# A two-layer decoder trunk on Trainium2: first norm vector by matrix products, first tile's halves taken apart, memory rows transposed once for both layers

## The chip, the core and the metric

The kernel runs on one core of a Trainium2 chip. The engines that work side by side are TensorE (PE: matrix products, and transposes as products with an identity), VectorE (DVE), ScalarE (ACT), GpSimd (POOL), and the DMA queues of SyncE (SP), ACT and POOL. The metric is the device time of one execution in microseconds, as the median of several runs. Before the change it is 1396.72 us (three runs, 1395.12 to 1397.05).

## What is computed

512 tokens of width 1024 go through two layers. Each layer is a mixer, a cross-attention into 256 memory tokens and a SwiGLU feed-forward block, and each of these stands between two RMS norms. The mixer of layer 0 is an attention with forget gates beside a short convolution; that of layer 1 is a gated linear recurrence.

```python
def rmsnorm(x, g):
    x32 = x.astype(jnp.float32)
    y = x32 * lax.rsqrt(jnp.mean(x32 * x32, axis=-1, keepdims=True) + EPS)
    return y.astype(x.dtype) * g
...
    for layer in range(DEPTH):
        h = rmsnorm(x, g_mix_pre[layer])
        ...
        x = x + rmsnorm(y, g_mix_post[layer])
        h = rmsnorm(x, g_cross_pre[layer])
        m = rmsnorm(mem, g_mem[layer])
        y = memory_cross_attention(h, m, w_xq[layer], w_xkv[layer], w_xo[layer])
        x = x + rmsnorm(y, g_cross_post[layer])
        h = rmsnorm(x, g_ffn_pre[layer])
        y = swiglu(h, w_ffn_gu[layer], w_ffn_down[layer])
        x = x + rmsnorm(y, g_ffn_post[layer])
```

The memory `mem` is the same in both layers; only the norm's gain `g_mem[layer]` (1024 numbers, one per channel) differs. All is float32.

## The kernel before

**Precision.** Every float32 product is made of three faster ones. An operand is split into a high part (a cast by ACT to the matmul's own format, `wh`, `hTh`, `mTh`) and a low part (operand minus high part, by DVE, `wl`, `hTl`, `mTl`). `mm3` (L318) adds high times high, high times low and low times high in one PSUM bank (L319 to L321).

**Layout.** The 512 tokens are four tiles `x[0]` to `x[3]` of 128 rows by 1024 channels, worked in two halves of 512 channels. `sumsq` (L218, ACT) or a DVE reduction (L242) sums the squares of a half; `rstd` (L220) makes the reciprocal root with two tiny DVE instructions (L222, L226) and a power on POOL (L230); `scaled` (L256, DVE) multiplies a half by it and by the gain. `put_T` (L299) transposes such a half in four products on PE (L303), and ACT (L312) and DVE (L313) split the result out of PSUM into `hTh` and `hTl`. The large tiles (`group`: four times 512 columns) share 14 slots.

**Order of the work.** PE takes its instructions in the order in which the code issues them. For ACT and DVE a scheduler decides the order, but for the first part of `fox` (L1198 to L1258), where they too follow the code. An engine works its list in order, so an instruction that waits holds up all behind it. All weights come over the SP queue through a ring of four buffers `st`. After a load, `pace` (L140) may let one of the `copies` go, which are transfers from DRAM to DRAM that prepare sums of the feed-forward weights (20 in each layer, planned at L677); `loads[0]` counts the loads, and a copy follows three of four loads once the count is above 0. The second operand of these sums is added by transfers of the POOL queue (L679).

**Start.** The norm's gain for the first tile comes in two ways. Half 0 is loaded as one row into `grow`, and a float32 product with a matrix `ones` (L1220, two passes in the trace) spreads it over the 128 partitions in a PSUM bank. Half 1 is loaded by SP with a transfer that writes it to all 128 partitions (`gain`, 256 KB). `warm_up` (L1176) runs products that nobody reads. Then both halves of tile 0 are transposed, and `mm_v` (L1189) makes the first products with the weights `st` (cast L1213, subtraction L1216): for the first two channel blocks "h" (high, high), "w" (high, low weights), "x" (low, high weights). Tile 1 follows after more products of tile 0.

**Memory.** In each layer `memory_rows` (L941) loads the four blocks of `mem` (L950), two by two sums their squares, and multiplies them by reciprocal root and gain (L956); the gain comes in two 256 KB transfers on the ACT queue (L107). `memory_T` (L961) returns two steps; each transposes one tile of 128 memory rows in eight products (L971) and splits them with two ACT casts (L976) and two DVE subtractions (L977). The steps run inside `half1` (L585), which makes the second half of the mixer's output projection: for each token tile 24 products, and after some of them `next` (row sums, norm) of the tile before and `transpose` of the one before that. Step 0 follows tile 0 and step 1 tile 1. `memory_kv` (L981) then needs `mTh` and `mTl`; its weights are `w_xkv`. Both layers call this at L1548 to L1549.

## Time and profile before

| what | value |
|---|---|
| median of three runs | 1396.72 us (1395.12 to 1397.05) |
| the profiled execution, its own time | 1394.71 us |
| its span, first to last instruction | 1392.9 us |
| what lies around the span | 1.8 us |
| mean granted clock of TensorE | 0.997 |
| PE busy | 1378.2 us, 99% of the span |
| DVE busy | 1116.3 us, 80% |
| ACT busy | 720.2 us, 52% |
| POOL busy | 111.1 us, 8% |
| DMA traffic | 233.61 MB, 168 GB/s on average |

The profile is one execution. A row of its timeline gives start and duration in us, the engine, the line of the code, the operation, output and inputs with shapes; "x4" is a group of four that ran one after the other, and "[1.05 <-DVE h L256]" says that the engine had been idle for 1.05 us, and what ended that. A row of its windows gives a stretch of time, then for PE, PEld, DVE, ACT and POOL the busy us with the number of instructions, the granted TensorE clock (1.00 is full), the share of the 16 DMA engines and the GB/s they moved. PE is counted as busy from start to modelled end, so a pipeline that is merely fed slowly looks busy too. 168 GB/s over the span is an average: the first 15 us move 287 GB/s.

### The profile page before, as it was taken

To read this page: it belongs to the slowest core of one execution; us is meant where nothing else is said; L and a number is where in the kernel's file an instruction comes from. 1 tells how busy PE (TensorE), PEld (TensorE's weight loads), DVE (VectorE), ACT (ScalarE), POOL (GpSimd) and SP (SyncE) were. 2 spreads that over 40 slices of the span, in tenths; PEclk is the share of its full clock that TensorE was granted. 3 is DMA by queue.
4 is the path that set the end of the run, shared out by engine and by line. 5 is a ranking of instruction groups with operands and counts; after the bars stand their busy time and mean duration, and the time that the engine had idled before them with its cause. 6 is when DMAs were issued, how large, how long until landed. Compare 5 with 4: busy or idle time off the path is not lost.

```text
span 1392.9 us, 21792 instructions
## 1 busy us (share of the span) xinstructions
PE 1378.2 (99%) x8432; PEld 1227.8 (88%) x8432; DVE 1116.3 (80%) x1801; ACT 720.2 (52%) x1175; POOL 111.1 (8%) x162
## 2 busy tenths in 40 slices
PE   8999999999999999999999999999999999999998
PEld 6778788888899999998879888888889999999886
DVE  6876678546589999989898998754558999999987
ACT  4354455534464444456664796543446444445663
POOL 1000001012010101000010000101200010000001
PEclk9999999999999999999999999999999999999999
DMA  6845452669224557567656657267822555656664
GB/s 224 277 155 159 137 181 57 202 164 177 66 92 142 163 143 196 160 241 222 195 159 210 222 181 242 73 199 163 164 67 91 166 150 151 177 168 233 205 188 144
DMA packets 156066, 233.61 MB, mean 168 GB/s; under 512 B 8549, under 2 KB 90545, under 8 KB 154938
## 3 DMA queue, kind: packets, MB, share of 16 engines
q1 hardware_dynamic: 135138, 180.25, 40.3%
q0 software_dynamic: 16928, 45.11, 15.0%
q10 hardware_dynamic: 3896, 6.86, 1.5%
q8 instruction: 66, 1.08, 0.3%
q14 instruction: 38, 0.31, 0.1%
HBM read 220.64 MB, written 57.69 MB: 200 GB/s over the span
## 4 chain that ended last, share of the span: by engine, by line
PE 95%; DVE 3%; issue 1%; DMA 1%; ACT 0%; POOL 0%; SPq 0%; DVEq 0%; POOLq 0%; ACTq 0%
PE bA L319 14%; PE bA L321 14%; PE bA L320 14%; PE bB L319 6%; PE bB L320 6%; PE bB L321 6%; PE bB L795 2%; PE bB L794 2%; PE bB L793 2%; PE bA L552 2%; PE bA L554 2%; PE bB L554 2%; PE bA L553 2%; PE bB L553 2%; PE bB L552 2%; PE bA L795 2%
## 5 line engine op out<-in xcount | busy, mean ns | idle before, releaser
L529 DVE TENSOR_TENSOR wl<-st,wh 128x1024 fp32r<-128x1024 f32 x108 | 131.4, 1222 | 99.1 <-ACT wh L528 98.1
L528 ACT CAST wh<-st 128x1024 fp32r<-128x1024 f32 x108 | 113.4, 1051 | 122.4 <-PE bA L320 70.6
L319 PE MATMUL bA<-hTh,wh 128*128 128x512 f32 (+1 forms) x448 | 171.9, 384 | 0.0
L321 PE MATMUL bA<-hTh,wl 128*128 128x512 f32 (+1 forms) x448 | 168.9, 377 | 2.3 <-DVE wl L781 2.3
L320 PE MATMUL bA<-hTl,wh 128*128 128x512 f32 (+1 forms) x448 | 168.2, 375 | 0.0
L420 ACT CAST wg<-wr 128x1024 fp32r<-128x1024 f32 x80 | 83.7, 1046 | 49.2 <-DVE wr L449 38.5
L759 ACT CAST wh<-st 128x1024 fp32r<-128x1024 f32 x76 | 74.9, 985 | 63.6 <-PE bA L795 27.0
L321 PEld LDWEIGHTS bA<-hTh,wl 128*128 128x128 f32 x448 | 84.8, 189 | 18.4 <-DVE wl L781 2.8
L421 DVE TENSOR_TENSOR wg<-wr,wg 128x1024 fp32r<-128x1024 f32 x80 | 97.4, 1217 | 0.0
L320 PEld LDWEIGHTS bA<-hTl,wh 128*128 128x128 f32 x448 | 85.0, 190 | 13.6
L319 PEld LDWEIGHTS bA<-hTh,wh 128*128 128x128 f32 x448 | 85.0, 190 | 13.4
L764 DVE TENSOR_TENSOR wl<-st,wh 128x1024 fp32r<-128x1024 f32 x76 | 86.7, 1140 | 10.1 <-ACT wh L759 10.1
L420 ACT CAST wh<-tt 128x1024 fp32r<-128x1024 f32 x40 | 42.1, 1053 | 61.5 <-DVE tt L449 61.5
L319 PE MATMUL bA<-hTq,wh 128*128 128x256 f32 x208 | 59.2, 284 | 0.0
L321 PE MATMUL bA<-hTq,wl 128*128 128x256 f32 x208 | 58.8, 283 | 0.0
L320 PE MATMUL bA<-hTq,wh 128*128 128x256 f32 x208 | 58.8, 283 | 0.0
L793 PE MATMUL bB<-wh,ya 128*128 128x512 f32 x148 | 57.6, 389 | 0.0
L794 PE MATMUL bB<-wl,ya 128*128 128x512 f32 x148 | 57.6, 389 | 0.0
L795 PE MATMUL bB<-wh,ya 128*128 128x512 f32 x148 | 57.6, 389 | 0.0
L739 DVE TENSOR_TENSOR ya<-yb,ya 128x512 fp32r<-128x512 f32 x84 | 53.9, 645 | 0.0
L793 PE MATMUL bA<-wh,ya 128*128 128x512 f32 x132 | 51.3, 389 | 0.0
L794 PE MATMUL bA<-wl,ya 128*128 128x512 f32 x132 | 51.3, 389 | 0.0
(372 smaller groups left out, 4434.8 us busy)
## 6 DMA issues: line engine op xcount, KB each, us to landing
wr<-in_w_ffn_gu_dram SPq DMA_DIRECT2D x80, 512.0 KB, 5.5
st<-t SPq DMA_DIRECT2D x40, 512.0 KB, 4.2
t<-in_w_ffn_down_dram SPq DMA_DIRECT2D x32, 512.0 KB, 5.1
st<-in_w_xkv_dram SPq DMA_DIRECT2D x32, 512.0 KB, 4.7
st<-in_w_ffn_down_dram SPq DMA_DIRECT2D x30, 512.0 KB, 3.4
st<-in_ab_w_in_dram SPq DMA_DIRECT2D x24, 512.0 KB, 4.7
y<-yr POOLq DMA_DIRECT2D x18, 512.0 KB, 4.2
t<-in_w_ffn_down_dram POOLq DMA_DIRECT2D x16, 512.0 KB, 8.4
```

Source lines behind the costliest of these rows:

```text
L319: nc.tensor.matmul(out=ps, lhsT=wh, rhs=xh, start=first, stop=False)
L320: nc.tensor.matmul(out=ps, lhsT=wh, rhs=xl, start=False, stop=False)
L321: nc.tensor.matmul(out=ps, lhsT=wl, rhs=xh, start=False, stop=last)
L420: return (lambda: nc.scalar.copy(out=to[0], in_=src), lambda: nc.vector.tensor_tensor(out=to[1], in0=src, in1=f(to[0]), op=ALU.subtract))
L421: lambda: nc.vector.tensor_tensor(out=to[1], in0=src, in1=f(to[0]), op=ALU.subtract))
L528: nc.scalar.copy(out=hi, in_=src)
L529: nc.vector.tensor_tensor(out=lo, in0=src, in1=f(hi), op=ALU.subtract)
L759: nc.scalar.copy(out=self.wt[s][0], in_=self.st[s])
L764: nc.vector.tensor_tensor(out=lo, in0=self.st[s], in1=f(hi), op=ALU.subtract)
L793: nc.tensor.matmul(out=banks[t], lhsT=yh, rhs=wh[:, jj, :], start=first and jj == 0, stop=False)
L794: nc.tensor.matmul(out=banks[t], lhsT=yh, rhs=wl[:, jj, :], start=False, stop=False)
L795: nc.tensor.matmul(out=banks[t], lhsT=yl, rhs=wh[:, jj, :], start=False, stop=last and jj == n - 1)
```

## The change

It has four parts, all in one diff.

**First gain.** Both halves of `g_mix_pre` come as rows of 2 KB, into partitions 0 and 32 of `grow`; the transfer to 128 partitions is gone. ACT casts `grow` to `growh`, DVE subtracts to `growl`, and four products with a selecting matrix `pick` put both halves into two PSUM banks. The row sums of tile 0 are issued with the DVE half ahead of `growl`.

**First tile.** Half 0 is transposed, the "h" and "w" products follow, then half 1 is transposed, then the "x" products.

**Memory.** The rows are normalised without the gain and transposed in layer 0 alone, into `raw` (a group named `mTr`). POOL's queue writes it to DRAM, `memT`, 1 MB. The gain of a layer is now one number per partition of the transposed layout (`chan`, column "gm", from 16 more rows loaded in `setup_chan`): for each of eight channel blocks ACT multiplies `raw` by it into `mTh`, and DVE makes `mTl` in one instruction. Layer 1 loads `memT` into its `raw` with one transfer on SP and has no loads of `mem`, no row sums and no transposes. The `gain` transfers of `g_mem` are gone in both layers.

**Copies.** The count of loads starts at -10, so the first of the copies follows ten loads later in layer 0.

```diff
@@ -86,10 +86,12 @@
     junk = const.tile([P, 512], BF16, name="junk")
-    grow = sbuf("grow")
-    ones = sbuf("ones", P)
+    grow, growh, growl, pick = sbuf("grow"), gains.tile([P, 512], F32R, tag="gain", name="growh"), \
+        gains.tile([P, 512], F32R, tag="gain", name="growl"), gains.tile([P, 512], F32R, tag="gain", name="pick")
     nc.vector.memset(grow, 0.0)
-    nc.vector.memset(ones, 1.0)
+    nc.vector.memset(f(pick)[:, 0:2 * P], 0.0)
+    for hf in range(2):
+        nc.vector.memset(f(pick)[32 * hf:32 * hf + 1, hf * P:hf * P + P], 1.0)
     nhalf = const.tile([P, 1], F32, name="nhalf")
@@ -160,6 +162,7 @@
         ("scw", a["ab_conv_w"][0].rearrange("j (m p) -> (j m) p", p=P)),
+        ("gm", a["g_mem"].rearrange("l (m p) -> (l m) p", p=P)),
     )
@@ -296,8 +299,8 @@
-    def put_T(hT, t, hs, bank=bankB):
-        for hf in range(2):
+    def put_T(hT, t, hs, bank=bankB, halves=range(2)):
+        for hf in halves:
             ps = bank()
@@ -938,10 +941,10 @@
-    def memory_rows(layer, gate):
-        with tc.issue_after(gate) if gate else nullcontext():
-            g = load_gain(a["g_mem"][layer])
+    memT = dram.tile([P, KT, MEM], F32, name="memT")
+    def memory_rows():
@@ -953,30 +956,46 @@
             for hf in range(2):
-                nc.vector.scalar_tensor_tensor(
-                    out=mt[hf], in0=mt[hf], scalar=r, in1=g[hf], op0=ALU.mult, op1=ALU.mult
-                )
+                nc.vector.tensor_scalar_mul(out=mt[hf], in0=mt[hf], scalar1=r)
         return mg
-    def memory_T(mg, bank):
+    def memory_T(layer, bank):
+        raw = f(group("mTr")).rearrange("p a (b c) -> p (a b) c", c=MEM)
         ghi, glo = group("mTh"), group("mTl")
...
-        def step(t):
+        if layer:
+            nc.sync.dma_start(out=raw, in_=memT)
+        else:
+            mg = memory_rows()
+        def turn(t):
             for hf in range(2):
...
                     )
-                v = ps.rearrange("p (k c) -> p k c", k=4)
-                dst = (slice(None), slice(hf * 4, hf * 4 + 4), slice(t * P, (t + 1) * P))
-                nc.scalar.copy(out=vhi[dst], in_=v)
-                nc.vector.tensor_tensor(out=vlo[dst], in0=v, in1=f(vhi[dst]), op=ALU.subtract)
-        return vhi, vlo, (lambda: step(0), lambda: step(1))
+                nc.scalar.copy(out=raw[:, hf * 4:hf * 4 + 4, t * P:(t + 1) * P], in_=ps.rearrange("p (k c) -> p k c", k=4))
+        def parts(ks):
+            for k in ks:
+                g = ch("gm", 8 * layer + k)
+                nc.scalar.mul(out=vhi[:, k, :], in_=raw[:, k, :], mul=g)
+                nc.vector.scalar_tensor_tensor(
+                    out=vlo[:, k, :], in0=raw[:, k, :], scalar=g, in1=f(vhi[:, k, :]), op0=ALU.mult, op1=ALU.subtract
+                )
+        def last():
+            turn(1)
+            nc.gpsimd.dma_start(out=memT, in_=raw)
+            parts(range(KT))
+        if layer:
+            return vhi, vlo, (lambda: parts(range(4)), lambda: parts(range(4, KT)))
+        return vhi, vlo, (lambda: turn(0), last)
@@ -1197,9 +1216,8 @@
             load_x(0)
-            nc.sync.dma_start(out=grow[0:1], in_=a["g_mix_pre"][0:1, 0:512])
-            g1 = gains.tile([P, 512], F32, tag="gain", name="gain")
-            nc.sync.dma_start(out=g1, in_=a["g_mix_pre"][0, 512:D].partition_broadcast(P))
+            for hf in range(2):
+                nc.sync.dma_start(out=grow[32 * hf:32 * hf + 1], in_=a["g_mix_pre"][0:1, hf * 512:hf * 512 + 512])
             raw = {}
@@ -1216,17 +1234,29 @@
             nc.scalar.activation(out=junk[:, 0:1], in_=nhalf, func=AF.Square)
-            g0 = bankB()
-            nc.tensor.matmul(out=g0, lhsT=ones, rhs=grow, start=True, stop=True)
-            g = g0, g1
+            nc.scalar.copy(out=growh, in_=grow)
+            g = bankB(), bankB()
+            st = stats("pre")
+            nc.vector.tensor_tensor_reduce(
+                out=sbuf("sq"), in0=x[0][:, 512:D], in1=x[0][:, 512:D], scale=1.0, scalar=0.0,
+                op0=ALU.mult, op1=ALU.add, accum_out=st[:, 1:2],
+            )
+            nc.vector.tensor_tensor(out=growl, in0=grow, in1=f(growh), op=ALU.subtract)
+            sumsq(x[0][:, 0:512], st[:, 0:1])
+            r = rstd(st)
+            for hf in range(2):
+                for i, part in enumerate((growh, growl)):
+                    nc.tensor.matmul(out=g[hf], lhsT=pick[:, hf * P:hf * P + P], rhs=part, start=i == 0, stop=i == 1)
             warm_up(WARM2)
-            r = row_stats(x[0], True)
             nc.vector.tensor_copy(out=identb, in_=ident)
...
             whi_v(0)
+            put_T(hT, 0, hs, halves=range(1))
             wlo_v(0)
-            put_T(hT, 0, hs)
-            mm_v(0, 0, "hwx")
+            mm_v(0, 0, "hw")
+            put_T(hT, 0, hs, halves=range(1, 2))
+            mm_v(0, 0, "x")
             whi_v(2)
@@ -1256,7 +1286,7 @@
                 mm_v(k0, 3)
-        loads[0] = 0
+        loads[0] = -10
         setup_chan()
@@ -1545,7 +1575,7 @@
             rglru(hT, prev, pm)
-        vhi, vlo, steps = memory_T(memory_rows(layer, pm.gate), pm.first)
+        vhi, vlo, steps = memory_T(layer, pm.first)
         pm.half1(steps)
```

At the program's start PE had this list (`grow,ones` is the gain's product, `ident,h` the transposes of `put_T`, `wh,hTh` the first weights):

```order
L1176 MATMUL bB<-ident 128x128 x13
L1220 MATMUL bB<-grow,ones 128x512
L1176 MATMUL bB<-ident 128x128 x4
L303 MATMUL bB<-ident,h 128x128 x8
L1189 MATMUL bA<-wh,hTh 128x512 x2
L1189 MATMUL bA<-wl,hTh 128x512 x2
L1189 MATMUL bA<-wh,hTl 128x512 x2
```

Now it has this:

```order
L1195 MATMUL bB<-ident 128x128 x13
L1250 MATMUL bB<-growh,pick 128x512
L1250 MATMUL bB<-growl,pick 128x512
L1250 MATMUL bB<-growh,pick 128x512
L1250 MATMUL bB<-growl,pick 128x512
L1195 MATMUL bB<-ident 128x128 x4
L306 MATMUL bB<-ident,h 128x128 x4
L1208 MATMUL bA<-wh,hTh 128x512 x2
L1208 MATMUL bA<-wl,hTh 128x512 x2
L306 MATMUL bB<-ident,h 128x128 x4
L1208 MATMUL bA<-wh,hTl 128x512 x2
```

The products for the gain are four in place of one, and the eight transposes are split in two lots of four, with the "h" and "w" products between them.

DVE at the same place, before (`x_110` is tile 0 and `x_111` tile 1; the first row makes the copy of the identity in bfloat16):

```order
L1224 CAST identb<-ident 128x128
L256 SCALAR_TENSOR_TENSOR h<-x_110,pre,bB 128x512
L256 SCALAR_TENSOR_TENSOR h<-x_110,pre,gain 128x512
L1216 TENSOR_TENSOR wl<-st,wh 128x1024
L313 TENSOR_TENSOR hTl<-bB,hTh 128x4x128 x2
L242 ISA sq,pre<-x_111 128x512
```

And now, where `x_114` and `x_115` are these tiles:

```order
L1252 CAST identb<-ident 128x128
L259 SCALAR_TENSOR_TENSOR h<-x_114,pre,bB 128x512 x2
L316 TENSOR_TENSOR hTl<-bB,hTh 128x4x128
L1234 TENSOR_TENSOR wl<-st,wh 128x1024
L316 TENSOR_TENSOR hTl<-bB,hTh 128x4x128
L245 ISA sq,pre<-x_115 128x512
```

The weights' subtraction stands between the two halves' subtractions instead of ahead of both, and the norm of both halves reads PSUM.

In layer 0, inside `half1`, DVE had this after the last update of tile 1, with what each waits for in brackets:

```order
L617 SCALAR_TENSOR_TENSOR x_111<-yb,post,x_111 128x512 [waits DVE_49]
L977 TENSOR_TENSOR mTl<-bA,mTh 128x4x128 [waits Activation_49] x2
L313 TENSOR_TENSOR hTl<-bA,hTh 128x4x128 [waits Activation_49] x2
L222 TENSOR_SCALAR pre<-pre 128x1 [waits Activation_49]
L226 SCALAR_TENSOR_TENSOR pre<-pre 128x1 [waits DVE_49,Activation_49]
L256 SCALAR_TENSOR_TENSOR h<-x_111,pre,gain 128x512 [waits Pool_49]
```

Now it is:

```order
L620 SCALAR_TENSOR_TENSOR x_115<-yb,post,x_115 128x512 [waits DVE_49]
L987 SCALAR_TENSOR_TENSOR mTl<-mTr,chan,mTh 128x256 [waits Activation_49] x8
L316 TENSOR_TENSOR hTl<-bA,hTh 128x4x128 [waits Activation_49]
L316 TENSOR_TENSOR hTl<-bA,hTh 128x4x128 [waits DMASW1_49,DVE_49,Activation_49]
L225 TENSOR_SCALAR pre<-pre 128x1 [waits Activation_49]
L229 SCALAR_TENSOR_TENSOR pre<-pre 128x1 [waits DVE_49,Activation_49]
L259 SCALAR_TENSOR_TENSOR h<-x_115,pre,gain 128x512 [waits Pool_49]
```

Two subtractions that read PSUM have become eight instructions that read `raw`. The second `hTl` now waits also for a semaphore of POOL's DMA queue (DMASW1) and for DVE's own: this tile takes the slot of `mTr`, so it waits until the write of `memT` has read it. On POOL that write stands ahead of the power of the next norm:

```order
L233 TENSOR_TENSOR post<-post,nhalf 128x1 [waits DVE_49]
L233 TENSOR_TENSOR pre<-pre,nhalf 128x1 [waits DVE_49,Pool_49]
L233 TENSOR_TENSOR post<-post,nhalf 128x1 [waits DVE_49]
L993 DMA memT<-mTr 128x2048 [waits Activation_49]
L233 TENSOR_TENSOR pre<-pre,nhalf 128x1 [waits DVE_49,Pool_49]
```

Before, the last row followed the first directly.

## The prediction

> **What bounds the kernel now.** I read first the page's chain of work that ended last, then the waits of PE, then busy time by windows.

> ```profile
> PE 95%; DVE 3%; issue 1%; DMA 1%; ACT 0%; POOL 0%; SPq 0%; DVEq 0%; POOLq 0%; ACTq 0%
> ```
> ```profile
> PE bB L303 <- DVE h L256: 2.5, 4, 1.1
> PE bA L321 <- DVE wl L781: 2.3, 2, 1.8
> ```
> ```profile
> 0.00:15.00 15.00, 10.50 (x40) 7.75 (x41) 7.96 (x18) 6.83 (x11) 3.15 (x11) 0.89 0.84 287
> 15.00:40.00 25.00, 24.73 (x120) 19.17 (x119) 17.03 (x28) 13.07 (x25) 2.01 (x2) 1.00 0.62 193
> 4.00:5.00 1.00, 1.00 (x5) 0.54 (x4) 0.72 (x3) 0.72 (x2) 0.00 (x0) 1.00 0.91 82
> 5.00:6.00 1.00, 0.82 (x5) 0.36 (x3) 0.43 (x3) 0.00 (x0) 0.52 (x1) 1.00 0.74 133
> 6.00:7.00 1.00, 0.13 (x1) 0.13 (x2) 0.75 (x1) 0.00 (x0) 0.03 (x1) 1.00 0.68 248
> 7.00:8.00 1.00, 0.58 (x5) 0.35 (x6) 0.75 (x1) 0.00 (x0) 0.00 (x0) 1.00 1.07 420
> 11.00:12.00 1.00, 1.00 (x3) 0.77 (x4) 1.00 (x3) 0.83 (x1) 0.00 (x0) 0.52 1.07 408
> 14.00:15.00 1.00, 1.00 (x5) 0.81 (x4) 0.56 (x2) 0.00 (x0) 0.76 (x1) 0.77 1.05 387
> ```

> PE carries 95% of the chain. Its waits are few: 2.5 us for the normalised rows at the very start and 2.3 us for a feed-forward weight, which this change doesn't touch. In the first 15 us PE is busy for 10.50; from 15 to 40 us for 24.73 of 25, with a clock of 1.00. So time can be won or lost in three ways only: by when PE comes to its steady work in the first 15 us, by instructions of PE that come or go, and by a new wait of PE in a place that is full now. Loads made earlier, and work taken from DVE or ACT elsewhere, are worth nothing.

> **The start.** The timeline of the first 16 us, cut to the rows that follow one another:

> ```profile
> 4.16 0.69 DVE L242 CUSTOM_DVE_ANT_0 sq<-x 128x512 f32<-128x512 f32 x1 [2.62 <-DMA x<-in_x_dram]
> 5.48 0.55 POOL L230 TENSOR_TENSOR pre<-pre,nhalf 128x1 f32<-128x1 f32 x1 [3.77 <-DVE identb L1224]
> 6.07 0.75 DVE L256 SCALAR_TENSOR_TENSOR h<-x,pre,bB 128x512 f32<-128x512 f32 x1 [0.61 <-POOL pre L230]
> 6.87 0.66 PE L303 MATMUL bB<-ident,h 128*128 128x128 f32 x4 [1.05 <-DVE h L256]
> 8.53 1.04 ACT L1213 CAST wh<-st 128x1024 fp32r<-128x1024 f32 x1 [3.58 <-DMA st<-in_ab_w_in_dram]
> 9.48 1.07 ACT L312 CAST hTh<-bB 128x512 fp32r<-128x512 f32 x2
> 9.61 1.23 DVE L1216 TENSOR_TENSOR wl<-st,wh 128x1024 fp32r<-128x1024 f32 x1 [1.72 <-ACT wh L1213]
> 10.11 0.73 PE L1189 MATMUL bA<-wh,hTh 128*128 128x512 f32 x2 [1.51 <-ACT hTh L312]
> 10.75 1.28 DVE L313 TENSOR_TENSOR hTl<-bB,hTh 128x512 fp32r<-128x512 f32 x2
> 10.89 1.11 PE L1189 MATMUL bA<-wl,hTh 128*128 128x512 f32 x2
> 12.12 0.62 ACT L218 ACTIVATE junk<-x 128x512 bf16<-128x512 f32 x1
> 13.29 1.47 POOL L230 TENSOR_TENSOR pre<-pre,nhalf 128x1 f32<-128x1 f32 x1 [7.26 <-DVE pre L226]
> 14.80 0.75 DVE L256 SCALAR_TENSOR_TENSOR h<-x,pre,bB 128x512 f32<-128x512 f32 x1 [0.45 <-POOL pre L230]
> 15.69 1.29 PE L303 MATMUL bB<-ident,h 128*128 128x128 f32 x8 [0.18 <-DVE h L256]
> ```

> What it removes: the transfer to 128 partitions. While it runs, the queues move 82, 133 and 248 GB/s in three windows, and 420 after; against 420 that is a loss of 0.81 + 0.68 + 0.41 = 1.9 us, and its own 256 KB take 0.6 us at 420. So the first weights land some 2.5 us earlier, and their cast starts at 6.0 in place of 8.53.

> What it adds ahead of the first product: `growl`, one DVE instruction of 128x512, at about the 0.69 of the row at 4.16, between the squares and the root. Some 0.1 of it lies in the wait for ACT's sum, so the norm starts at 6.07 + 0.55 = 6.6, the transposes of half 0 at 7.4, and end at 8.06; one cast (half of 1.07) ends at 8.6. The first product moves from 10.11 to 8.6. The four products for the gain take the place of an idle PE there.

> That gain of 1.5 us isn't kept, by what follows. The low weights come after the first `hTl` on DVE: 8.6 + 0.64 + 1.23 = 10.5 for the two "w" products (10.89 before). Now half 1 is transposed only after these, and ACT's list has its cast ahead of the second weights and of tile 1's squares. Step by step: two products 0.65 (between 0.45, two steps at full clock, and the 0.85 that the pairs take in the window with clock 0.52), to 11.2; four transposes 0.8 (0.66, and more at half clock), to 12.0; cast 0.54, to 12.5; second `wh` 1.04, to 13.6; squares, tiny instructions and all up to POOL's start 1.17 (from 12.12 to 13.29), to 14.7; POOL's power 1.47, to 16.2; norm to transposes 0.9 (14.80 to 15.69). Tile 1's transposes start at 17.1 in place of 15.69. All of tile 0's products fit ahead of that, and PE is full behind it, so the 1.4 us remain. **Term: +1.4.** What would hide it is other work for PE, and there is none, since tile 0 has no more channels cast. Below, the first product's whole gain of 1.5 is kept; above, a second such power or a half clock adds as much again: −1.5 to +2.9.

> The power is the largest piece. It takes 0.55 at 5.48, when DVE is idle but for a small cast, and 1.47 beside the weights' subtraction; in the new order this subtraction again lies beside it, so I take 1.47; at 0.55 the term is +0.5. [...]

> **Layer 0, memory.** The timeline around tile 1 of the output projection, a DVE instruction of 128x256 for its size, and then what POOL's transfers of 1 MB take, from the DMA issues and from the view of their line:

> ```profile
> 33.89 0.42 DVE L529 TENSOR_TENSOR wf<-st,wf 128x256 fp32r<-128x256 f32 x1
> 220.19 0.60 ACT L218 ACTIVATE junk<-bB 128x512 bf16<-128x512 f32 x1 [0.79 <-PE bB L554]
> 220.78 1.07 ACT L976 CAST mTh<-bA 128x512 fp32r<-128x512 f32 x2
> 222.09 0.15 DVE L226 SCALAR_TENSOR_TENSOR post<-post 128x1 f32<-128x1 f32 x1
> 223.57 0.75 DVE L617 SCALAR_TENSOR_TENSOR x<-yb,post,x 128x512 f32<-128x512 f32 x1
> 225.43 1.28 DVE L313 TENSOR_TENSOR hTl<-bA,hTh 128x512 fp32r<-128x512 f32 x2
> 227.77 1.42 DVE L256 SCALAR_TENSOR_TENSOR h<-x,pre,gain 128x512 f32<-128x512 f32 x2 [0.73 <-POOL pre L230]
> 229.91 1.03 PE L303 MATMUL bA<-ident,h 128*128 128x128 f32 x8
> ```
> ```profile
> yb<-y POOLq DMA_DIRECT2D x8, 1024.0 KB, 5.4
> ```
> ```profile
> DMA to landing us min/median/max: 5.0/5.4/9.4
> ```

> PE's instructions stay the same here. On DVE, step 0 loses its two subtractions, so the chain of tile 1 no longer stands behind them: its first tiny instruction follows ACT's squares, which end at 220.79, with some 0.15 for the reading of the sum: 220.95 in place of 222.09, and the update of `x` ends 1.14 earlier than 224.32, at 223.2. Then come eight instructions of 128x256 at 0.40 apart (0.42 alone): 3.2 us, to 226.4. The eight multiplications on ACT run ahead of them, from 221.85. The first `hTl` ends at 227.0. The second one waits for the write of `memT`, issued on POOL when the copies out of PSUM end, 221.85. The nearest rows are POOL's 1 MB reads, 5.4 in the median and 9.4 at most: landing at 227.3, or 231.3. With the first, `hTl` ends at 227.9, the norm follows 1.06 later as now (226.71 to 227.77), at 229.0, its first half is there at 229.75 and the second at 230.4. PE wants them at 229.91 and, four transposes on, at 230.3: **+0.1**. With the second, all is 4.0 later: +4.1. Below, 0, as PE loses no instruction. [...]

> **Layer 1, memory.**

> ```profile
> 849.76 1.88 SPq L950 DMA_DIRECT2D mem<-in_mem_dram  x4
> 856.69 0.63 ACT L531 ACTIVATE y<-ge 128x512 fp32r<-128x512 f32 x1 [0.26 <-DVE ge L1513]
> 864.79 0.39 PE L552 MATMUL bB<-wh,y 128*128 128x512 f32 x1
> 872.96 1.04 PE L971 MATMUL bB<-ident,mem 128*128 128x128 f32 x8
> 873.75 0.47 PE L552 MATMUL bA<-rh,y 128*128 128x512 f32 x1
> ```

> Two lots of eight transposes go, each 873.75 − 872.96 = 0.79 of PE's time, and the product after each is about 0.1 longer than its 0.39 neighbours: 2 × 0.9, **−1.8**. PE is full there, so this is won in full if nothing waits. The new load of 1 MB takes the place of the four loads at 849.76 and lands at 855.2 (5.4) to 859.2 (9.4). ACT's eight multiplications stand ahead of the cast of the last `y` at 856.69, which PE needs at 864.79: even from 859.2, and at the 0.54 that a cast twice their size takes, they end at 863.5 and `y` at 864.1. So this wait costs nothing; the DVE half follows later and has lost more than it gained. Bounds: −1.9 to −1.6.

> **Edits at nothing.** The copies that start ten loads later still run before the feed-forward block that reads them, and no wait of PE after 15 us is for a transfer; the cover is the whole cross-attention between. Without it a copy costs its landing, some 5 us each, once. The 16 more rows of gains and the absent 256 KB gain loads lie on ACT's queue, with nothing behind them that waits.

> **Sum.** +1.4 + 0.1 − 1.8 = −0.3. The profiled execution took 1394.71 (span 1392.9 and 1.8 around it), 2.0 less than the median of the three runs, 1396.72: the same sum gives 1394.4 on the one and 1396.4 on the other. I forecast the median: **1396.4**. A measurement of this kernel can tell about 0.2% from no change, 2.8 us, so this is no change.

> **The rivals.**

> *The first product's gain is kept* (faster). If POOL's power is short this time, and tile 1's chain goes with the first weights as it does before, the start gives −1.5 and not +1.4, and the sum is −3.2: 1393.5; with the full 2.5 us of the earlier weights −4.2: 1392.5. For it: PE waits 1.51 for `hTh` at 10.11, and that does go. Against it: the new round trip over ACT between half 0 and half 1. Chance 0.17.

> *The write of `memT` holds DVE* (slower). It lies in layer 0, where the second `hTl` waits in DVE's list with tile 1's norm behind it, and PE behind that. At the 9.4 landing the sum is −0.3 + 4.0: 1400.4. It decides from a landing 8.6 us after the issue, where the total passes +2.8. [...] Against: the median 5.4, and DMA has little to do around 220 us. Chance 0.16.

> *The clock* (about the same, or slower). In the window from 11 to 12 the clock was 0.52, and from 14 to 15 it was 0.77, so half clock lasted from 11.0 to some 14.4: 3.4 us. PE idles differently at the start, between 8.06 and 10.5. One more such stretch under full work costs half of it, 1.7: 1398.1; two 1399.8. [...] Chance 0.14, 0.07 of it slower.

> That the change doesn't do what it says is not open for layer 1: the transposes are not in PE's list.

> **How the numbers follow.** My forecast has 0.53; it lies within 0.2%, with its own range of 1395.0 to 1398.0. The rivals have 0.17, 0.16 and 0.14. Of the first 0.16 passes the bound of 2.8 us; of the second, all but little. So faster 0.16, within 0.2% 0.62, slower 0.22. The range reaches to the fast rival's lower end, 1392.5, and to the slow one's 1400.4.

> **What would show it.** In the profile after: the first product near 8.6; tile 1's transposes near 17.1 and POOL's power ahead of them near 1.5; the second `hTl` of tile 0 in layer 0 released by the transfer near 227.3 (all later by the start's shift), with a wait of PE for `h` under 0.5; no transposes of memory in layer 1, and no wait of PE there. I am wrong if PE waits in layer 0 for more than 2 us, if tile 1's transposes start before 15, or if the clock falls again after 20 us.

## The result and the profile after

The changed kernel takes 1398.23 us in the median of 22 runs (1396.77 to 1400.74); the kernel before, in as many runs beside it, takes 1395.78 (1394.71 to 1398.0). The ratio is 1.0017, with a 95% interval of 1.001 to 1.0023: 2.4 us slower. The forecast was 0.3 faster. The profiled execution of the changed kernel has a span of 1395.4 us against 1392.9, 2.4 more before rounding.

To see where they go, I took the start of each product of PE in one trace and of the same product in the other; the difference is called the shift. At 22 us it is +2.65, at 100 us +3.4, at 260 us +3.5, at 760 us +3.7, at 900 us +1.9, and at the last product +2.1 (1387.79 against 1385.71). So the start loses 2.6, something near 73 us loses 0.75, layer 1's memory wins 1.85, and the rest is small; between the last product and the end another 0.35 lies in the output's transfers.

The chain that ended last, and the first of PE's waits, of the changed kernel:

```profile
PE 91%; issue 3%; DVE 3%; DMA 1%; ACT 1%; POOL 0%; DVEq 0%; POOLq 0%; SPq 0%; ACTq 0%
```
```profile
PE bA L324 <- DVE pre L225: 1.9, 2, 1.3
PE bA L324 <- DVE wl L784: 1.8, 1, 1.8
PE bA L1208 <- ACT wh L1231: 1.5, 2, 1.2
PE bB L1195 <- POOL ident masks.py:199: 1.5, 1, 1.5
PE bA L1208 <- DVE wl L1234: 1.1, 1, 1.1
```

The first two stand where the wait for feed-forward weights stood before, at the border of the layers. New are the waits of L1208, the first tile's products: for the casts of the next two weights (1.15 and 0.36 us), and for the first low weights between "h" and "w". The timeline of the start after (L1231 cast of weights, L306 transposes, L259 norm):

```profile
8.05 1.05 ACT L1231 CAST wh<-st 128x1024 fp32r<-128x1024 f32 x1 [2.63 <-DMA st<-in_ab_w_in_dram]
9.63 0.73 PE L1208 MATMUL bA<-wh,hTh 128*128 128x512 f32 x2 [0.70 <-ACT hTh L315]
11.49 0.73 PE L1208 MATMUL bA<-wl,hTh 128*128 128x512 f32 x2 [1.12 <-DVE wl L1234]
12.06 0.60 PE L306 MATMUL bB<-ident,h 128*128 128x128 f32 x4
12.69 0.58 ACT L315 CAST hTh<-bB 128x512 fp32r<-128x512 f32 x1 [3.11 <-PE bB L306]
13.17 1.05 ACT L1231 CAST wh<-st 128x1024 fp32r<-128x1024 f32 x1
15.30 1.47 POOL L233 TENSOR_TENSOR pre<-pre,nhalf 128x1 f32<-128x1 f32 x1 [8.79 <-DVE pre L229]
16.80 1.41 DVE L259 SCALAR_TENSOR_TENSOR h<-x,pre,bB 128x512 f32<-128x512 f32 x2 [0.44 <-POOL pre L233]
17.70 1.93 PE L306 MATMUL bB<-ident,h 128*128 128x128 f32 x8
```

Tile 1's transposes start at 17.70 in place of 15.69. The weights' cast starts only 0.48 earlier than before, and the chain behind it is the one that was forecast. The eight transposes take 1.93 in place of 1.29: the granted clock was 0.50 there. The windows of the changed kernel, with the DMA's share and GB/s at the end of each row:

```profile
4.00:5.00 1.00, 0.66 (x4) 0.26 (x2) 0.88 (x3) 0.82 (x2) 0.00 (x0) 1.00 0.40 117
5.00:6.00 1.00, 1.00 (x2) 0.56 (x3) 0.90 (x4) 0.42 (x2) 0.04 (x1) 1.00 0.92 223
6.00:7.00 1.00, 1.00 (x3) 0.63 (x3) 0.46 (x1) 0.00 (x0) 0.51 (x1) 1.00 0.95 322
12.67:16.08 3.41, 1.89 (x7) 0.94 (x7) 2.47 (x6) 3.09 (x5) 0.78 (x1) 1.00 0.74 231
16.08:19.49 3.41, 3.41 (x13) 2.55 (x13) 1.74 (x4) 0.59 (x1) 0.69 (x1) 0.50 0.56 153
```

Without the transfer to 128 partitions the queues still reach only 117, 223 and 322 GB/s in the windows from 4 to 7 us, where it was 82, 133 and 248. And the half clock lies from 16.08 to 19.49, where PE has work for every moment. Before, it lay from 11.0 to 14.4 (0.51): PE was busy there too, but with products that were done before tile 1's norm, for which PE still waited 0.18 at 15.69.

The clock of 1.00 that the profile prints ahead of 9.23 us is not a measured one: the trace's record of the clock begins only there (at 4.21 in the kernel before), and what lies ahead is printed as full. The four unread products of 128x128 show the difference, in the changed kernel and then in gain_only (below), whose record begins at 5.14:

```profile
7.02 1.05 PE L1195 MATMUL bB<-ident 128*128 128x128 f32 x4
```
```profile
6.53 0.60 PE L1178 MATMUL bB<-ident 128*128 128x128 f32 x4
```

So the changed kernel's PE was still slow in this execution through the products for the gain and half 0's transposes, four of which took 1.06 and ended at 8.93, where four took 0.60 at 12.06.

### The profile page after: what moved, and what is told of

Read it like the earlier page. It is cut to its first block, busy times and chain, and to the rows that moved or that the text cites. A ratio compares the mean times of both kernels' runs of the same rounds, so it can differ in the third digit from the quotient of the medians.

```text
span 1395.4 us, 21752 instructions
## 1 busy us (share of the span) xinstructions
PE 1378.0 (99%) x8418; PEld 1226.6 (88%) x8418; DVE 1115.4 (80%) x1804; ACT 722.1 (52%) x1180; POOL 111.8 (8%) x161
## 3 DMA queue, kind: packets, MB, share of 16 engines
q0 software_dynamic: 17072, 46.16, 15.1%
## 4 chain that ended last, share of the span: by engine, by line
PE 91%; issue 3%; DVE 3%; DMA 1%; ACT 1%; POOL 0%; DVEq 0%; POOLq 0%; SPq 0%; ACTq 0%
PE bA L322 13%; PE bA L324 13%; PE bA L323 13%; PE bB L322 6%; PE bB L323 6%; PE bB L324 6%; PE bB L797 2%; PE bB L798 2%; PE bB L796 2%; PE bA L557 2%; PE bA L555 2%; PE bB L557 2%; PE bB L555 2%; PE bA L556 2%; PE bB L556 2%
## 5 line engine op out<-in xcount | busy, mean ns | idle before, releaser
L531 ACT CAST wh<-st 128x1024 fp32r<-128x1024 f32 x108 | 113.2, 1050 | 119.5 <-PE bA L323 67.8
L324 PEld LDWEIGHTS bA<-hTh,wl 128*128 128x128 f32 x448 | 84.3, 188 | 19.7 <-DVE wl L784 4.3
L323 PEld LDWEIGHTS bA<-hTl,wh 128*128 128x128 f32 x448 | 84.5, 189 | 13.6
```

The source lines that it names most:

```text
L323: nc.tensor.matmul(out=ps, lhsT=wh, rhs=xl, start=False, stop=False)
L324: nc.tensor.matmul(out=ps, lhsT=wl, rhs=xh, start=False, stop=last)
L531: nc.scalar.copy(out=hi, in_=src)
```

## The experiments

Theory A at first: taking the halves of tile 0 apart makes the loss, by the longer chain of waits to tile 1's transposes, and some of it by the half clock that now lies over full work. Rivals: B, the gain by products makes it; C, the copies or the memory part make it; D, for the step near 73 us, the new rows of gains or the shifted start.

Each edited kernel was timed beside the kernel before, in 8 to 11 runs, but the last, of which there is one run. The table gives each kernel's shift against the profiled kernel before at 22 us, its steps between 65 and 100 us, between 210 and 260 us (memory in layer 0), between 700 and 760 us (border of the layers) and between 850 and 900 us (memory in layer 1), all read from one trace each, and the ratio of the timed runs. The profiled run of the kernel before, 1394.71, is the fastest of its 22, so the shifts against it come out larger than the times.

| kernel | 22 us | 73 us | layer 0 | border | layer 1 | ratio (95%) |
|---|---|---|---|---|---|---|
| changed kernel | +2.65 | +0.75 | +0.15 | +0.22 | −1.85 | 1.0017 (1.0010 to 1.0023) |
| old_start | +1.05 | +0.95 | +0.12 | +0.20 | −1.86 | 0.9995 (0.9986 to 1.0004) |
| halves_together | −0.59 | +0.49 | +1.64 | +0.56 | −1.85 | 0.9995 (0.9987 to 1.0004) |
| copies_0 | +3.80 | +0.21 | +1.40 | +1.51 | −1.89 | 1.0016 (1.0007 to 1.0025) |
| memory_only | +0.02 | +0.32 | +0.12 | +1.51 | −1.87 | 0.9997 (0.9988 to 1.0006) |
| split_only | +5.01 | +0.23 | 0.00 | +0.21 | 0.00 | 1.0025 (1.0015 to 1.0035) |
| half1_before_w | +3.27 | +0.47 | +0.12 | +0.21 | −1.89 | 1.0019 (1.0010 to 1.0028) |
| act_write | −0.36 | +1.07 | 0.00 | +1.59 | −1.89 | 0.9983 (0.9974 to 0.9992) |
| best0 | −0.35 | +0.24 | +0.01 | +1.50 | −1.89 | 0.9982 (0.9973 to 0.9991) |
| after_fill | +2.14 | +0.67 | 0.00 | +1.45 | −1.89 | 1.0003 (0.9995 to 1.0012) |
| half1_fill | +1.17 | +0.79 | 0.00 | +1.52 | −1.86 | 0.9995 (0.9986 to 1.0004) |
| gain_only | −0.07 | +0.08 | 0.00 | +1.73 | −0.01 | 0.9992 (0.9984 to 1.0001) |
| copies_only | −0.14 | +0.64 | 0.00 | +0.20 | 0.00 | one run |

**old_start.** Start as before, memory and copies as changed.

```diff
-            for hf in range(2):
-                nc.sync.dma_start(out=grow[32 * hf:32 * hf + 1], in_=a["g_mix_pre"][0:1, hf * 512:hf * 512 + 512])
+            nc.sync.dma_start(out=grow[0:1], in_=a["g_mix_pre"][0:1, 0:512])
+            g1 = gains.tile([P, 512], F32, tag="gain", name="gain")
...
-            put_T(hT, 0, hs, halves=range(1))
...
+            put_T(hT, 0, hs)
+            mm_v(0, 0, "hwx")
```

> The changed kernel with the start of before (row and broadcast load for the gain, both halves of tile 0 transposed together); memory rows and the later copies stay as changed. Theory A (the loss is made in the start by the halves taken apart: tile 1's transposes 2.0 us later and the half-clock stretch then lying over full work, 0.6 more): tile 1's transposes come back to 15.7, the shift of PE against before is 0 at 20 us, +0.7 after 73 us (wait for the running sums of the forget gates), and about -0.7 at the end: 0.6 to 1.0 us faster than before, 2.6 to 3.2 faster than the changed kernel. Rival C (the copies or the memory part cost the 2.6 somewhere, the start's shift being chance of that execution): the time stays near that of the changed kernel, 2 us slower than before.

The loss is gone (0.9995), so it is made in the start. A shift of 1.05 was left there in this trace, where none was expected. It begins with the first weights, whose cast starts at 9.56 in place of 8.53:

```profile
9.56 1.04 ACT L1230 CAST wh<-st 128x1024 fp32r<-128x1024 f32 x1 [4.59 <-DMA st<-in_ab_w_in_dram]
```

The time was 0.2 faster than before by the medians and 0.7 by the ratio; its interval, from 2.0 faster to 0.6 slower, neither shows nor excludes the 0.6 to 1.0 expected.

**halves_together.** The edit within the start that is undone:

```diff
-            put_T(hT, 0, hs, halves=range(1))
             wlo_v(0)
-            mm_v(0, 0, "hw")
-            put_T(hT, 0, hs, halves=range(1, 2))
-            mm_v(0, 0, "x")
+            put_T(hT, 0, hs)
+            mm_v(0, 0, "hwx")
```

> The changed kernel with one edit undone: both halves of tile 0 are transposed together ahead of the first products, as before; the gain still comes by products. Theory A (splitting the halves costs the start): the first product stays near 9.7, tile 1's transposes come at 15.2 to 15.7, the shift at 20 us is -0.4 to 0, and the time is 0.7 to 1.2 us faster than before. Rival B (the gain by products costs the start: growl ahead of the root, products ahead of the transposes): tile 1's transposes stay near 17.7, and the time stays 2 to 2.5 us slower than before.

The shift at 22 us is −0.59: the gain by products costs nothing, and taking the halves apart makes the loss. Between the two ratios lie 0.0022, 3.1 us. The expected gain over before, 0.7 to 1.2, isn't clear of the noise (from 1.8 faster to 0.6 slower); this trace has a new step of 1.64 in layer 0:

```profile
222.03 0.59 POOL L993 DMA_DIRECT2D memT<-mTr  x1 [0.44 <-ACT mTr L981]
228.50 0.69 DVE L316 TENSOR_TENSOR hTl<-bA,hTh 128x512 fp32r<-128x512 f32 x1 [1.70 <-DMA memT<-mTr]
231.17 1.29 PE L306 MATMUL bA<-ident,h 128*128 128x128 f32 x8 [1.21 <-DVE h L259]
```

The write of `memT` landed 6.3 us after its issue, DVE stood 1.70 for it, and PE 1.21 for the norm behind. In the changed kernel's own trace it landed after 4.8, and DVE waited 0.19:

```profile
225.52 0.59 POOL L993 DMA_DIRECT2D memT<-mTr  x1 [0.44 <-ACT mTr L981]
230.49 0.69 DVE L316 TENSOR_TENSOR hTl<-bA,hTh 128x512 fp32r<-128x512 f32 x1 [0.19 <-DMA memT<-mTr]
```

**copies_0 and copies_only.** One number in the changed kernel and in the kernel before.

```diff
-        loads[0] = -10
+        loads[0] = 0
```

> The changed kernel with the count of loads starting at 0 as before, all else as changed. Theory A (the later copies run beside the write and the loads of the running sums near 65 to 70 us, and this costs PE 0.7 at 73 us): no step of the shift at 73 us, 0.7 us faster than the changed kernel, 1.5 to 1.8 slower than before. Rival D (the step at 73 us comes from the new rows of gains in the set-up or from the shifted start): the step of 0.7 stays, and so does the time.

> The kernel before with one number changed, the count of loads from -10. Theory (the later copies run beside the write and the loads of the running sums): a step of 0.4 to 1.0 of PE's shift near 73 us and a wait of PE for DVE there, nothing else. Rival (the step comes from the new gain rows or the shifted start): no step above 0.3.

The step near 73 us fell from 0.75 to 0.21 with the count from 0, and rose to 0.64 when that number alone was put into the kernel before. In the eight traces with −10 it is 0.47 to 1.07, in the five that start at 0 it is 0.08 to 0.32. The rows are the loads `cb` of the running sums, on POOL's queue, their first use, and PE's wait behind it, of the changed kernel and then, without such a wait, of the kernel before:

```profile
70.19 1.13 POOL L1352 DMA_DIRECT2D cb<-cum  x2 [4.14 <-DMA cum<-e]
75.11 0.29 DVE L1374 CUSTOM_DVE_ANT_0 p<-bB,cb 128x128 f32<-128x128 f32 x1 [6.24 <-DMA cb<-cum]
76.15 0.79 PE L1367 MATMUL bB<-qk 64*128 64x384 f32 x5 [0.24 <-DVE fx L1374]
```
```profile
65.68 1.13 POOL L1322 DMA_DIRECT2D cb<-cum  x2 [2.26 <-DMA cum<-e]
71.56 0.29 DVE L1344 CUSTOM_DVE_ANT_0 p<-bB,cb 128x128 f32<-128x128 f32 x1 [5.31 <-DMA cb<-cum]
```

POOL waits 4.14 in place of 2.26 for the write `cum` to land, DVE for the loads, and PE for DVE. That the copies' own traffic delays the write fits, but which transfer it is was not tried. In the time of copies_0 this half microsecond is not to be seen: its trace lost 1.40 in layer 0 and 1.51 at the border. Its shift at 22 us is 3.80 where the changed kernel, with the same start, has 2.65: its first weights came 0.47 later, and PE was slow for longer. The record of the clock begins only at 20.28 in this trace, and pairs of products took 1.05 ahead of it and 0.63 behind:

```profile
17.52 1.05 PE L1208 MATMUL bA<-wh,hTh 128*128 128x512 f32 x2
21.08 0.63 PE L1208 MATMUL bA<-wh,hTh 128*128 128x512 f32 x2
```

**memory_only.** The changed kernel with the start as in old_start, and the copies as before.

```diff
-            put_T(hT, 0, hs, halves=range(1))
...
+            put_T(hT, 0, hs)
+            mm_v(0, 0, "hwx")
...
-        loads[0] = -10
+        loads[0] = 0
```

> The kernel before with the memory part alone: start and copies as before. Theory A: shift of PE against before 0 until layer 1, -1.8 there by the two lots of transposes, 1.5 to 1.8 us faster than before. Rival (the memory part costs as much in layer 0, by the transfer that the second low half waits for, or by the 1 MB load in layer 1): no difference, or slower.

The 1.87 of layer 1 are there, and the ratio is 0.9997. The time fits the rival's "no difference", but not for its reasons: the step in layer 0 is 0.12, and the trace loses 1.51 at the border of the layers, which gain_only, without the memory part, loses too. Theory A isn't excluded: the interval reaches from 1.7 faster to 0.8 slower.

**split_only.** The kernel before with the halves taken apart, the reverse of the edit in halves_together.

```diff
-            put_T(hT, 0, hs)
-            mm_v(0, 0, "hwx")
+            put_T(hT, 0, hs, halves=range(1))
+            wlo_v(0)
+            mm_v(0, 0, "hw")
+            put_T(hT, 0, hs, halves=range(1, 2))
+            mm_v(0, 0, "x")
```

> The kernel before with one part of the change alone: half 0 of tile 0 transposed, "h" and "w" products, half 1 transposed, "x" products. Theory A (this order alone makes the loss, by the chain low weights, products, half 1, cast, second weights, squares, power, norm): tile 1's transposes at 17.5 to 18.5 in place of 15.7, a stretch of half clock between 15 and 20 us, shift of PE 2.0 to 2.7 at 22 us and to the end, 2.0 to 2.7 us slower than before. Rival B (only together with the gain by products): a shift under 0.7, and no difference in time.

This one part alone costs 0.25%, 3.5 us, where the whole change cost 2.4. That is theory A's direction, but more than its 2.0 to 2.7; tile 1's transposes start at 20.41 and not by 18.5. In its trace the first weights came late (cast at 9.69), and the clock was 0.50 from 11.30 to 21.53:

```profile
7.89:11.30 3.41, 0.03 (x1) 0.03 (x1) 0.80 (x2) 1.53 (x2) 0.00 (x0) 1.00 1.04 407
11.30:14.71 3.41, 2.77 (x7) 1.75 (x8) 1.78 (x2) 0.00 (x0) 0.00 (x0) 0.50 1.04 398
14.71:18.12 3.41, 2.64 (x8) 1.73 (x7) 1.95 (x6) 2.88 (x5) 0.26 (x1) 0.50 0.87 279
18.12:21.53 3.41, 3.41 (x12) 2.64 (x12) 2.20 (x3) 0.24 (x2) 1.21 (x1) 0.50 0.45 122
```

**half1_before_w.** Half 1 ahead of the "w" products.

```diff
-            wlo_v(0)
-            mm_v(0, 0, "hw")
+            mm_v(0, 0, "h")
             put_T(hT, 0, hs, halves=range(1, 2))
-            mm_v(0, 0, "x")
+            wlo_v(0)
+            mm_v(0, 0, "wx")
```

> The changed kernel with half 1 of tile 0 transposed after the "h" products and ahead of the "w" products, so that the halves stay apart but the low weights are no longer in the chain to half 1. Theory A (the wait for the low weights between the halves is what costs): tile 1's transposes at 15.5 to 16.2, shift at 22 us 0 to 0.5, and a time 0.5 faster to 0.5 slower than before, about 2.4 faster than the changed kernel. Rival E (any order with the halves apart loses, since half 1's cast stands ahead of the second weights on ACT): transposes after 16.8, at least 1.2 us slower than before.

Theory A as first stated failed here: the chain got shorter, the time didn't (1.0019). The norm of tile 1 is ready almost a microsecond earlier than in the changed kernel, and PE comes to its transposes later:

```profile
13.49 1.22 PE L1208 MATMUL bA<-wl,hTh 128*128 128x512 f32 x2 [2.53 <-DVE wl L1234]
15.89 1.41 DVE L259 SCALAR_TENSOR_TENSOR h<-x,pre,bB 128x512 f32<-128x512 f32 x2 [0.45 <-POOL pre L233]
18.78 1.43 PE L306 MATMUL bB<-ident,h 128*128 128x128 f32 x8
```
```profile
9.39:12.80 3.41, 1.17 (x6) 0.80 (x6) 1.88 (x3) 2.15 (x4) 0.00 (x0) 0.99 1.05 407
12.80:16.21 3.41, 2.72 (x6) 2.15 (x7) 2.93 (x7) 1.28 (x3) 1.47 (x1) 0.50 0.68 206
16.21:19.62 3.41, 3.41 (x12) 2.71 (x11) 1.08 (x2) 0.00 (x0) 0.00 (x0) 0.51 0.54 154
```

PE waits 2.53 for the low weights; the window of 3.41 us that holds most of this has 1.17 of work, and the next two run at half clock. Rival E's numbers came (transposes after 16.8, more than 1.2 us slower), but not for its reason, since the cast on ACT isn't what is late. So a third theory, H: the gap itself costs, by the clock.

**after_fill and half1_fill.** Products that nobody reads fill the gaps, on PE alone; what the kernels compute is the same. The cut shows half1_fill against half1_before_w's order; after_fill has 4 ahead of the first product, 8 between "h" and "w" and 8 behind "x".

```diff
+        def fill(n):
+            bank = bankB()
+            for _ in range(n):
+                nc.tensor.transpose(out=bank[:, 0:P], in_=ident, identity=ident)
...
+            fill(4)
             mm_v(0, 0, "h")
             put_T(hT, 0, hs, halves=range(1, 2))
+            fill(18)
             wlo_v(0)
```

> The changed kernel with 20 products more that nobody reads, on PE alone, in the gaps of the start: 4 ahead of the first product, 8 between "h" and "w", 8 after "x". They leave every other engine's order as it is. Theory H (the gaps on PE bring a stretch of half clock onto the work behind them, in the changed kernel 0.6 of the 2.6): with the gaps filled no half clock between 9 and 22 us, tile 1's transposes at 17.3 to 17.7 as the norm's chain sets them, shift at 22 us 1.8 to 2.1, time 0.5 to 0.9 faster than the changed kernel. Theory A (only the chain of waits counts): shift stays at 2.6.

> The kernel with half 1 transposed ahead of the "w" products, with 4 products that nobody reads ahead of the first product and 18 after half 1's transposes. Theory H: that kernel's norm of tile 1 was ready 1.1 us later than before (15.89 against 14.80), and the other 2.3 of its shift of 3.4 came from the half clock between 12.9 and 19.7; with the gap filled the clock stays at 1.00, tile 1's transposes come at 16.5 to 17.0, the shift at 22 us is 0.9 to 1.4, and the time is about 2 us faster than without the filling, near that of before. Theory A: the shift stays above 2.5.

Theory H holds in both. In half1_fill the clock stays at 1.00 from the record's begin at 10.01, and the transposes follow the norm:

```profile
15.98 1.41 DVE L259 SCALAR_TENSOR_TENSOR h<-x,pre,bB 128x512 f32<-128x512 f32 x2 [0.45 <-POOL pre L233]
16.87 1.29 PE L306 MATMUL bB<-ident,h 128*128 128x128 f32 x8 [0.28 <-DVE h L259]
```

Shift 1.17 in place of 3.27, and 0.9995 in place of 1.0019, 3.3 us. In after_fill the shift is 2.14 in place of 2.65, just above the 1.8 to 2.1 expected, and the time fell by 2.0 (1.0003 against 1.0017, with intervals that overlap by 0.0002), more than the 0.5 to 0.9 expected and more than its trace shows. A trace shows one execution, and the half clock doesn't lie at the same place in each (11.96 in memory_only's trace, 11.04 before); the timed runs may hold others. A start as slow as that of copies_0 (1400.04) would be one of these; the changed kernel's four slowest runs took 1400.3 to 1400.74, but no trace shows their starts.

**act_write and best0.** Halves together, and the write on ACT's queue; best0 also counts the loads from 0.

```diff
-            nc.gpsimd.dma_start(out=memT, in_=raw)
+            nc.scalar.dma_start(out=memT, in_=raw)
```

> The kernel with the halves together and the write of memT on ACT's queue in place of POOL's. Theory F (in layer 0 the second low half waits for this write, which lands 4.8 to 6.3 us after its issue on POOL's queue; PE loses 1.0 to 1.2 when it is 6 and nothing when it is 4.8): on ACT's queue it lands within 4.8, PE doesn't wait for h at 230 us in this profile, and the time is 0.7 to 1.3 us faster than before. Rival G (the landing is the same on any queue, or the issue holds up ACT's multiplications): a step of 0.3 or more at 230 us, no faster than with the write on POOL.

> As the kernel with the write on ACT's queue and the halves together, and the count of loads from 0 as before. Theory: what the memory part wins in layer 1 (1.85) and the start (0.5) is kept but for the layer boundary, and the step at 73 us is 0 to 0.3 and not 0.5 to 0.9: 1.2 to 2.0 us faster than before, 0.1 to 0.15%. Rival: the copies make no difference, the time is that of the kernel with the write on ACT's queue; or the wait at the layer boundary near 735 us takes back what is won, and no difference to before is left.

In act_write the write landed after 4.5 (best0's trace doesn't show its landing), and neither trace has a step in layer 0. But on POOL it landed between 4.2 and 6.3, so this doesn't show that the queue is the reason. Both kernels are faster than the kernel before, by 2.4 and 2.5 us; that is more than the 0.7 to 1.3 and 1.2 to 2.0 expected, though the intervals reach down to 1.1 and 1.3. Between them the time shows no difference. Against halves_together act_write is 0.0012 faster, about as much as the interval of either.

**gain_only.** The kernel before with the gain by products and nothing else.

```diff
-            nc.tensor.matmul(out=g0, lhsT=ones, rhs=grow, start=True, stop=True)
-            g = g0, g1
+            for hf in range(2):
+                for i, part in enumerate((growh, growl)):
+                    nc.tensor.matmul(out=g[hf], lhsT=pick[:, hf * P:hf * P + P], rhs=part, start=i == 0, stop=i == 1)
```

> The kernel before with the gain by products alone: halves together, memory and copies as before. Expected by all theories: first product near 9.7, tile 1's transposes at 15.1 to 15.5, shift at 22 us -0.3 to -0.6, kept to the end but for the layer boundary; 0.3 to 1.0 faster than before, less than a measurement tells. If the gain by products costs: a shift above 0.

The shift at 22 us is −0.07, smaller than expected; the time is 0.08% lower, with an interval that just holds 1.

## Why the prediction was wrong, point by point

- *"So the first weights land some 2.5 us earlier"*: this is where the start's working first failed. They came 0.48 earlier (8.05 against 8.53). I had read the low rates from 4 to 7 us as the cost of one transfer; with it gone they are still 117 to 322 GB/s. Over all traces the cast starts at 8.39 to 9.69 with the transfer (five) and at 7.82 to 8.52 without it (nine). Half 0's transposes were late as well: they ended at 8.93 and not at 8.06, since the products ahead of them ran slowly (1.05 for the four unread ones, where 0.60 had been the pace before). First product at 9.63 and not 8.6.
- *The chain between the halves* was right in mechanism and in most terms. From "w" to tile 1's transposes I worked out 6.6 us; it took 6.2 (11.49 to 17.70). POOL's power took 1.47, as taken. With "w" 1.0 later than I had it (11.49 against 10.5) and the chain 0.4 shorter it gives +2.0, not +1.4, inside the range of −1.5 to +2.9, and after_fill, with full clock from 10.69 on, has 2.14.
- *The clock* I had put among the rivals at 0.14 as chance and at nothing in the sum; by the timed runs this was the larger error. A window in which PE was busy for 1.89 of 3.41 us was followed by half clock (0.50 from 16.08 to 19.49), and the new order itself opens the gaps: the half clock cost 0.5 to 0.65 us in this trace and about 2 by the timed runs with and without filling.
- *Layer 0*: +0.1 forecast, 0.15 measured, and the landing (5.4 taken) was 4.8. The rival's mechanism is real: at 6.1 and 6.3, in two of eight traces with that write, it cost 1.4 and 1.6. It never came near 9.4.
- *Layer 1*: −1.8 forecast, −1.85 to −1.89 in every trace that has it, with no wait of PE for the new load.
- *"no wait of PE after 15 us is for a transfer"*: wrong. PE waited for DVE, and DVE for the loads of the running sums; the copies that I moved at no cost made this some 0.5 longer.
- *The border of the layers* I left out. I had also put the chain's 2.5 us of waits for normalised rows all at the very start, though 0.84 of it lies here, in the row below. The first wait here is as before (1.81 against 1.80), but the clock behind it is not: the step is 0.2 to 0.56 with one window of half clock, as in the kernel before, or none, and 1.45 to 1.73 with two. Kernels with and without each changed part stand in both groups, so none of the parts sets it.

```profile
743.23 1.23 PE L303 MATMUL bB<-ident,h 128*128 128x128 f32 x8 [0.84 <-DVE h L256]
```

The sum that the changed kernel's trace gives is +2.65 + 0.75 + 0.15 + 0.22 − 1.85 and small steps of 0.16, 2.08 at the last product, where I had −0.3. Of the 2.4 between them the start is 1.25 (+2.65 for +1.4) and the copies, put at nothing, 0.75. What stays open: how the loss of the start divides between the chain and the clock, by the trace mostly the chain and by the timed runs mostly the clock, since only mean clocks of the timed runs are known, and these leave out what lies ahead of the record; and why the first weights came a microsecond late in old_start and split_only.

## What to carry to other kernels

Where PE is nearly always busy, as here (99% of the span), a change of order is judged by the gaps that it opens on PE and by what work comes in the 3.41 us behind them, which ran at a clock of 0.50 in the changed kernel, not only by the chain of waits; some twenty unread products in a gap can be worth more than a shorter chain, as in half1_fill against half1_before_w (3.3 us). A wait of PE that names DVE is followed one step further before a transfer is called free to move. When an early transfer is slow, look at what the queues do without it before its removal is counted as time won.

## What the hardware showed that was not expected

```profile
9.26:12.67 3.41, 1.92 (x9) 1.35 (x10) 1.82 (x2) 0.32 (x1) 0.00 (x0) 1.00 1.04 405
```

At the border of the layers, too, windows with 1.61 us of work (the kernel before, best0) and 1.65 (gain_only) were followed by half clock, and one with 1.63 (halves_together) by full clock. One of each kind with the window behind it, from halves_together and then from gain_only:

```profile
729.07:732.48 3.41, 1.63 (x9) 1.21 (x8) 3.21 (x6) 0.43 (x1) 1.15 (x1) 1.00 0.00 0
732.48:735.89 3.41, 2.12 (x16) 1.91 (x17) 2.78 (x5) 2.25 (x5) 0.41 (x2) 1.00 0.46 154
```
```profile
728.76:732.18 3.42, 1.65 (x13) 1.49 (x12) 2.94 (x6) 0.31 (x1) 1.40 (x1) 1.00 0.11 13
732.18:735.59 3.41, 2.13 (x11) 1.96 (x10) 3.26 (x7) 3.38 (x7) 0.55 (x1) 0.50 0.90 310
```

So the busy time that the profile shows does not decide it alone. At half clock, windows with 2.58 us busy (best0), 2.64 and 2.77 (split_only) and 2.72 (half1_before_w) were followed by another at half, and those with 2.91 (the kernel before, at the border), 3.40 (best0) and 3.41 (the starts of both kernels, half1_before_w and split_only) by full clock. The half clock does not begin at the same point of the program in each execution: memory_only has the start of before and a shift of 0.02 at 22 us, and its half clock begins at 11.96 where that of the kernel before begins at 11.04. So what a gap costs need not be the same in each. The four traces with the products for the gain and with the halves together (halves_together, act_write, best0, gain_only) show a clock of 1.00 in every us from 9 to 22, where the kernel before has 3.4 us of half clock.
